# A list schedule that keeps TensorE on products of one kind, whole-array or part-array

## The chip, the cores and the metric

The kernel runs on one core of a Trainium2 chip. The metric is device time in microseconds (us), the median of several executions. The engines of a core work side by side, each through its own instructions in their fixed order: TensorE (PE, matrix products into PSUM), VectorE (DVE), ScalarE (ACT), GpSimd (POOL) and the queue that issues transfers (SP).

## The reference

Two layers over 1,024 tokens of width 1,024, in float32. Each layer modulates and normalizes x, projects it once, runs three mixers side by side on the columns of that projection, projects back and ends with a gated feed-forward part:

```
for l in range(DEPTH):
    mod = jax.nn.silu(c) @ ada_w[l] + ada_b[l]
    ...
    h = rms_norm(x, norm1_g[l]) * (1.0 + sc1) + sh1
    z = h @ w_in[l]
    ...
    o_a = dsa_mixer(...)      # attention to the 256 best keys of an indexer
    o_b = rwkv7_mixer(...)    # a recurrence over the tokens, 8 heads of 64
    o_c = nsa_mixer(...)      # compressed, selected and windowed attention
    mixed = jnp.concatenate([o_a, o_b, o_c], axis=-1) @ w_out[l]
    x = x + g1 * mixed
    h = rms_norm(x, norm2_g[l]) * (1.0 + sc2) + sh2
    gate, up = jnp.split(h @ ffn_wi[l], 2, axis=-1)
    x = x + g2 * ((jax.nn.silu(gate) * up) @ ffn_wo[l])
```

## The kernel before

Tokens are worked in halves of 512, and the work of different halves, mixers and layers is woven together: many generators (streams) yield pieces of work, a planner decides whose piece comes next, and every instruction is recorded with its number in this trace (`r.n`), its engine, its operands and its cost. Buffers in SBUF and PSUM are given out in that step, so what depends on what is fixed by it.

`Program.order()` then makes the final order. It is a list schedule: a model of the chip (`Chip`) says when each engine is free; of the instructions that are ready on an engine, the one with the lowest number in the trace is taken. The engine that can start first goes next, and `Chip.put` moves the model's clock on. The result is one order for each engine; the chip follows it whether or not the model's times were right. An instruction whose operand is late holds up all that stands behind it on its engine.

Products on TensorE come in two kinds for this model. A product has a range of 32-row strips and one of 32-column strips of the 128x128 array (`r.pe`). It is **whole** when it takes four of both, and **part** otherwise. Whole are the projections and the feed-forward (`mm`, three products of float32r halves for each float32 one: `hh`/`hl` by `whi`/`wlo`), the attention scores `at` and the transposes `pt`, `tk`. Part are the products of the recurrence in 64x64 blocks (`X`, `TX`, `WU`, `PT`, `MN`, `S`, `av`, `am`) and in 128x64 (`Y`, the second half of `MN`), attention by values `po` (128x64) and sums over partitions `ssk`, `ss` (128x32). `Chip.start` charges 0.095 us for going from whole to part and 0.045 us for going back, and `Chip.put` another 0.105 us for the first whole one after a part one. So the model knows what a change of kind costs, and the choice among ready products does not look at it.

A part product of the recurrence appears in the profile as two instructions (8 recorded products of `PT` as x16).

Of the kernel before, what the change touches and what calls it, by code (L numbers as in the profile page):

```python
# [88 lines left out]
def consts():  # L89
# [6 lines left out]
    p = np.arange(128)[:, None]  # L96
    f = np.arange(128)[None, :]
    put("ident", p == f)

    put("mask", np.concatenate([np.where(f > p, 0.0, NEG), np.zeros((128, 384)), np.where(f <= p, 0.0, NEG)], 1))  # L100
    put("one", np.ones((128, 1)))
    w = np.arange(32)[None, :]
    put("blkw", p // 64 == w // 16)
# [417 lines left out]
class Program:  # L521
# [83 lines left out]
    def order(self):  # L605


        recs, chip = self.recs, Chip()
        missing = [len(r.deps) for r in recs]
        for r in recs:  # L610
            for d in r.deps:
                recs[d].users.append(r.n)
        ready = {e: [] for e in ENGINES}
        coming = {e: [] for e in ENGINES}
        at = [0.0] * len(recs)
        for r in recs:
            if not missing[r.n]:
                heapq.heappush(coming[r.key], (0.0, r.n))
        out = []
        while len(out) < len(recs):  # L620
            best = None
            for e in ENGINES:
                t = chip.free[e]
                if not ready[e]:
                    if not coming[e]:
                        continue
                    t = max(t, coming[e][0][0])
                while coming[e] and coming[e][0][0] <= t:
                    heapq.heappush(ready[e], heapq.heappop(coming[e])[1])
                n = ready[e][0]  # L630
                s = max(chip.start(recs[n]), at[n])
                if s > t + 0.1 and recs[n].port:

                    for m in heapq.nsmallest(8, ready[e])[1:]:
                        if not recs[m].port and t + recs[m].cost < s + 0.1:
                            n, s = m, max(t, at[m])
                            break
                if best is None or s < best[0]:
                    best = (s, e, n)
            s, e, n = best  # L640
            if ready[e][0] == n:
                heapq.heappop(ready[e])
            else:
                ready[e].remove(n)
                heapq.heapify(ready[e])
            end = chip.put(recs[n], s)
            out.append((s, n))
            for u in recs[n].users:
                v = recs[u]
                at[u] = max(at[u], chip.after(recs[n], v, s, end))  # L650
                missing[u] -= 1
                if not missing[u]:
                    heapq.heappush(coming[v.key], (at[u], u))
        self.span = max(chip.free.values())
        self.starts = {n: s for s, n in out}
        out.sort()
        return [recs[n] for _, n in out]

    def issue(self, tc, order, pools, inputs):
        nc = tc.nc  # L660
        engines = {"PE": nc.tensor, "V": nc.vector, "S": nc.scalar, "G": nc.gpsimd, "D": nc.sync}
        made = {}

        def real(x):
            if not isinstance(x, bass.AP):
                return x
            name = x.tensor.name
            t = made.get(name)
            if t is None:
                b = self.born.get(name)  # L670
                if b is None:
                    t = inputs[name]
                elif b.tag is None:
                    t = pools[b.pool].tile(b.shape, b.dt, name=b.name)
                else:
                    t = pools[b.pool].tile(b.shape, b.dt, name=b.name, tag=b.tag, bufs=1)
                made[name] = t
            h = t.tensor if t.dtype == x.dtype else t.bitcast(x.dtype).tensor
            return bass.AP(tensor=h, offset=x.offset, ap=x.ap)

        with tc.manual_schedule():
            for r in order:
                getattr(engines[r.key], r.name)(*[real(x) for x in r.a], **{n: real(x) for n, x in r.k.items()})  # L683
# [5 lines left out]
class Chip:  # L689
# [5 lines left out]
    def __init__(self):  # L695
# [3 lines left out]
        self.port, self.wire, self.table, self.ring = 0.0, 0.0, None, [0.0] * 8  # L699
        self.stretch, self.work, self.over, self.slow, self.lost = 0, 0.0, 0.0, False, 0.0  # L700

    def start(self, r):

        t = self.free[r.key]
        if r.key == "PE":
            rows, cols, _ = r.pe
            part = rows[1] - rows[0] + cols[1] - cols[0] < 8
            for i in range(*rows):
                t = max(t, max(self.cells[i][cols[0]:cols[1]]))
            return t + (0.0 if part == self.part else 0.095 if part else 0.045)  # L710
        if r.key == "D":
            return max(t, self.ring[0])
        return max(t, self.port - 0.14) if r.port else t

    def put(self, r, s):

        if r.key == "PE":
            rows, cols, c = r.pe
            while s >= (self.stretch + 1) * self.STRETCH:
                share, self.work = (self.work + min(self.over, self.STRETCH)) / self.STRETCH, 0.0  # L720
                self.over = max(0.0, self.over - self.STRETCH)
                self.slow = share < (self.HIGH if self.slow else self.LOW)
                self.stretch += 1
            part = rows[1] - rows[0] + cols[1] - cols[0] < 8
            more = 0.105 if not part and self.first else 0.0

            step = c if not part or r.a[1].dtype != F32 else c / 2 + (0.0 if self.first else 0.05)
            if part and cols[1] - cols[0] == 1:
                step = 0.014
            self.first = part  # L730
            share = 1.0 if not part else (rows[1] - rows[0]) * (cols[1] - cols[0]) / 16.0
            if self.slow:
                self.lost += c * (share if share > 0.3 else 0.3)
                c, step = c * 2, step * 2
            self.work += c if not part else c * max(0.3, share)
            if not part or step < 0.05:
                for i in range(*rows):
                    self.cells[i][cols[0]:cols[1]] = [s + c + more] * (cols[1] - cols[0])
            self.part = part
            self.free["PE"] = s + step + more  # L740
            return s + c
        if r.key == "D":
            self.free["D"] = s + r.cost
            size = r.a[0].free_size() * r.a[0].partition_size() * 4
            self.wire = max(self.wire, s + r.cost) + size / 390e3
            self.ring = self.ring[1:] + [self.wire + 1.5]
            return self.wire + 1.5
        c = r.cost
        if r.func in (AF.Exp, AF.Silu) and r.func != self.table:
            self.table, c = r.func, c + 1.28  # L750
        if r.port:
            self.port = s + c
        self.free[r.key] = s + c - OVER[r.key]
        return s + c
# [17 lines left out]
def trace(ctx: ExitStack, tc: tile.TileContext, A, out, layers=L, plan=None, program=None):  # L772
# [97 lines left out]
    def mm(o, l, r, start=True, stop=True, **kw):  # L870
        o, l, r = flat(o), flat(l), flat(r)
        n = 1
        for x in r.shape[1:]:
            n *= x
        m = l.shape[-1]
        if r.dtype == F32:
            c = 2 * max(2 * n / 2400.0 + (0.0045 if n < 256 else 0.04), m * 0.00083 if m > 32 else 0.05)
        else:
            c = (n if n >= 256 else 4 * n) / 2400.0 + 0.0136
        array(c, (o, l, r), l, l.shape[0], o, m)  # L880
        if program is None:
            PE.matmul(o, l, r, start=start, stop=stop, **kw)
        else:
            program.add("PE", "matmul", (o, l, r), dict(start=start, stop=stop, **kw), (o, l, r), (o,), c, cells)
# [1562 lines left out]
    def mods():  # L2447
        yield from until(("v0",0,0))
        for l in range(layers):
# [7 lines left out]
          [("C", l, b) for b in range(4 * h, 4 * h + 4)] + [("A", l, b) for b in range(4 * h, 4 * h + 4)]]  # L2457
    rq = [(l, p, h) for l in range(layers) for h in range(2) for p in range(4)]
    wv.run((PR["main"], start(0)), (PR["mod"], consts_()), (PR["main"], start(1)), (PR["main"], main()), (PR["mod"], mod_round(0, 0, 16)), *[(PR["att"], att_worker(aq)) for _ in range(NA)],
           (PR["rw"], rw_worker(rq)), (PR["rw2"], rw_worker(rq, lambda t: (t[0], t[2]) in ((0,0),(1,0),(1,1)))),  # L2460
           (PR["mod"], mods()))
# [44 lines left out]
```

## Time and profile before

| what | value |
|---|---|
| median of 3 runs | 3489.34 us (3488.12 to 3493.7) |
| the profiled execution | 3489.09 us |
| its span, first to last instruction | 3487.3 us |
| TensorE busy | 3276.2 us, 94% of the span |
| VectorE busy | 2184.3 us, 63% |
| ScalarE busy | 1781.6 us, 51% |
| GpSimd busy | 1494.4 us, 43% |
| mean granted TensorE clock | 0.97 of full speed |

Busy time of TensorE includes what a product spends in filling and emptying the array. Since products overlap, the time that one costs is read from the start of one to the start of the next.

### The profile page before, as it was taken

How to read it: one execution, taken by the hardware profiler on the slowest of the kernel's cores; microseconds unless marked ns; L12 is line 12 of the kernel's file. 1: busy time of each engine (PE TensorE's matmuls, PEld its weight loads, DVE VectorE, ACT ScalarE, POOL GpSimd, SP SyncE). 2: the span in 40 equal slices, each digit the busy share in tenths (PEclk: the TensorE clock that was granted, in tenths of full speed). 3: DMA queues.
4: the chain of work that ended last, by engine and by line, in shares of the span. 5: the costliest groups of instructions: out<-in, count | busy, mean ns of one | idle time of the engine just before them, and what ended most of it. 6: DMA issues, size and time to landing. Idle time of an engine off the chain costs nothing. (4 is left out here: it accounts for less than half of the span.)

```text
span 3487.3 us, 58649 instructions
## 1 busy us (share of the span) xinstructions
PE 3276.2 (94%) x20564; PEld 2478.0 (71%) x20564; DVE 2184.3 (63%) x5705; ACT 1781.6 (51%) x3708; POOL 1494.4 (43%) x1235
## 2 busy tenths in 40 slices
PE   7889899989999998999899998999899999999999
PEld 3646666766777776677677886667677777778887
DVE  4688878889889624699962114688877843251112
ACT  3445556666674643545563334557777455343232
POOL 3423343433345344453444554443243344445554
PEclk8999999998999998999999999999899999999999
DMA  8674345545623243554223333553222222433333
GB/s 283 196 238 130 90 134 161 156 129 152 200 83 109 66 128 107 151 165 124 75 79 103 97 97 107 152 179 117 63 79 74 75 79 76 134 98 99 97 97 97
DMA packets 354755, 424.99 MB, mean 122 GB/s; under 512 B 129686, under 2 KB 167190, under 8 KB 354460
## 3 DMA queue, kind: packets, MB, share of 16 engines
q1 hardware_dynamic: 354460, 421.25, 39.7%
q8 instruction: 162, 2.65, 0.3%
q14 instruction: 133, 1.09, 0.1%
HBM read 347.06 MB, written 60.44 MB: 117 GB/s over the span
## 5 line engine op out<-in xcount | busy, mean ns | idle before, releaser
L683 POOL TENSOR_TENSOR wlo<-wraw,whi 128x512 fp32r<-128x512 f32 (+1 forms) x808 | 1071.7, 1329 | 1354.7 <-ACT whi L683 1229.3
L683 ACT ACTIVATE whi<-wraw 128x512 fp32r<-128x512 f32 (+1 forms) x808 | 500.7, 621 | 993.9 <-PE mm L683 663.5
L683 PE MATMUL mm<-hh,whi 128*128 128x512 f32 x2144 | 873.7, 409 | 27.6 <-ACT hh L683 10.3
L683 PE MATMUL mm<-hh,wlo 128*128 128x512 f32 x2128 | 845.9, 398 | 7.5 <-POOL wlo L683 7.4
L683 PE MATMUL mm<-hl,whi 128*128 128x512 f32 x2112 | 843.0, 399 | 7.5 <-POOL hl L683 3.8
L683 PEld LDWEIGHTS mm<-hh,whi 128*128 128x128 f32 x2144 | 408.7, 191 | 143.7 <-issue 26.7
L683 PEld LDWEIGHTS mm<-hh,wlo 128*128 128x128 f32 x2128 | 406.3, 191 | 99.9 <-POOL wlo L683 11.7
L683 PEld LDWEIGHTS mm<-hl,whi 128*128 128x128 f32 x2112 | 403.8, 191 | 96.1 <-issue 8.8
L683 DVE TENSOR_TENSOR sg<-sg,mm 128x512 f32<-128x512 f32 x87 | 59.6, 685 | 478.2 <-PE mm L683 478.0
L683 DVE SCALAR_TENSOR_TENSOR x<-mm,mod,x 128x512 f32<-128x512 f32 x232 | 172.9, 747 | 258.6 <-PE mm L683 258.0
L683 PE MATMUL mm<-acthi,whi 128*128 128x512 f32 x704 | 279.4, 402 | 9.3 <-ACT acthi L683 5.0
L683 PE MATMUL mm<-actlo,whi 128*128 128x512 f32 x704 | 277.1, 396 | 2.8 <-POOL actlo L683 2.7
L683 PE MATMUL mm<-acthi,wlo 128*128 128x512 f32 x704 | 275.1, 394 | 0.0
L683 ACT ACTIVATE p<-p,nb,rst 128x512 f32<-128x512 f32 (+3 forms) x256 | 170.7, 668 | 81.7 <-DVE nb L683 80.9
L683 ACT ACTIVATE junka<-score,tk_nt 128x512 int8<-128x512 f32 x240 | 166.4, 693 | 29.0 <-DVE tk_nt L683 22.9
L683 ACT COPY pT<-pt 128x512 f32<-128x512 f32 (+2 forms) x220 | 124.9, 584 | 102.4 <-PE pt L683 96.8
L683 PEld LDWEIGHTS mm<-acthi,whi 128*128 128x128 f32 x704 | 132.6, 189 | 48.7 <-issue 8.0
L683 PEld LDWEIGHTS mm<-actlo,whi 128*128 128x128 f32 x704 | 133.0, 189 | 33.9 <-POOL actlo L683 7.6
L683 DVE TENSOR_SCALAR p<-p,rs 128x512 f32<-128x512 f32 (+3 forms) x288 | 153.7, 586 | 0.7
L683 PEld LDWEIGHTS mm<-acthi,wlo 128*128 128x128 f32 x704 | 133.0, 189 | 27.8 <-issue 0.8
L683 PE MATMUL pt<-c_ident,p 128*128 128x128 f32 x816 | 136.8, 282 | 8.9 <-DVE p L683 7.9
L683 PE MATMUL po<-pT,tm 128*64 128x256 f32 x816 | 132.6, 407 | 6.7 <-ACT pT L683 6.5
(386 smaller groups left out, 5900.8 us busy)
## 6 DMA issues: line engine op xcount, KB each, us to landing
wraw<-in_wi_dram SPq DMA_DIRECT2D x352, 256.0 KB, 2.6
ada<-in_ada_dram SPq DMA_DIRECT2D x192, 256.0 KB, 4.6
wraw<-in_win_dram SPq DMA_DIRECT2D x184, 256.0 KB, 3.1
wraw<-in_wo_dram SPq DMA_DIRECT2D x160, 256.0 KB, 2.6
x<-x SPq DMA_DIRECT2D x64, 256.0 KB, 3.7
w<-in_w_dram SPq DMA_DIRECT2D x64, 256.0 KB, 3.7
wraw<-in_wout_dram SPq DMA_DIRECT2D x64, 256.0 KB, 2.7
o_in<-o SPq DMA_DIRECT2D x32, 256.0 KB, 3.5
```

The costliest lines, as they stand in the source:

```text
L683: getattr(engines[r.key], r.name)(*[real(x) for x in r.a], **{n: real(x) for n, x in r.k.items()})
```

## The change

When the lowest-numbered ready product on TensorE is of the other kind than the last one issued, `order()` now looks for the lowest-numbered ready product of the same kind, and takes it if its number in the trace is at most 100 above. The record of kinds is kept in two heaps, `kinds`; what has been issued is in `begun`. The model's prices, the records, the buffers and what depends on what are as before.

```
-        recs, chip = self.recs, Chip()
+        recs, chip, LATER = self.recs, Chip(), 100
+        kinds, begun = ([], []), set()
...
-                    heapq.heappush(ready[e], heapq.heappop(coming[e])[1])
+                    n = heapq.heappop(coming[e])[1]
+                    heapq.heappush(ready[e], n)
+                    if e == "PE":
+                        heapq.heappush(kinds[Chip.is_part(recs[n])], n)
                 n = ready[e][0]
+                if e == "PE" and Chip.is_part(recs[n]) != chip.part:
+                    same = kinds[chip.part]
+                    while same and same[0] in begun:
+                        heapq.heappop(same)
+                    if same and same[0] - n <= LATER:
+                        n = same[0]
...
+            if e == "PE":
+                begun.add(n)
...
+    @staticmethod
+    def is_part(r):
+        rows, cols, _ = r.pe
+        return rows[1] - rows[0] + cols[1] - cols[0] < 8
```

What this does to the order was counted over all of TensorE's 16,312 recorded products. A return trip is one stretch of part products between whole ones.

| counted in TensorE's order | before | now |
|---|---|---|
| return trips whole, part, whole | 610 | 326 |
| changes from one part shape to another (64x64, 128x64, 128x32, 64x128) | 148 | 266 |

By place in the program, marked by the time at which the same whole products ran before (return trips removed; part-to-part changes added): 0 to 200 us 21; 2. 200 to 1000 us 86; 54. 1000 to 1300 us 44; 20. 1300 to 1500 us 13; 0. 1500 to 1800 us 35; 24. 1800 to 2100 us 4; 0. 2100 to 2550 us 34.5; 7. 2550 to 2900 us 38.5; 11. From 2900 us on 8; 0. A part product stands on average 13 products later in the order than it did, a whole one 5 earlier; nine in ten of the part products are at most 34 places later.

The first place is about 1162 us into the run, on TensorE: `TX` is a part product of the recurrence, `pt` are whole transposes of the attention, and 13 recorded `TX` stand in one row as x13. Before:

```order
4505 L683 MATMUL mm_13433<-hh_9363,whi_13317 128x512
4506 L683 MATMUL TX_13475<-Tt_13297,X_13466 64x64
4507 L683 MATMUL pt_13419<-c_ident,p_13305 128x128
4508 L683 MATMUL TX_13475<-Tt_13297,X_13466 64x64 x2
4509 L683 MATMUL pt_13419<-c_ident,p_13326 128x128
4510 L683 MATMUL TX_13475<-Tt_13297,X_13466 64x64 x13
4511 L683 MATMUL pt_13421<-c_ident,p_13305 128x128
```

The same products of TensorE in the changed kernel:

```order
4515 L697 MATMUL mm_13394<-hh_9360,whi_13424 128x512
4516 L697 MATMUL pt_13472<-c_ident,p_13188 128x128
4517 L697 MATMUL TX_13475<-Tt_13292,X_13461 64x64 x16
4518 L697 MATMUL pt_13455<-c_ident,p_13267 128x128
4519 L697 MATMUL pt_13455<-c_ident,p_13297 128x128
```

Three stretches of `TX` have become one, and two return trips are gone; the transposes that stood between them now follow.

The second place is on TensorE some 20 products on, where attention by values (`po`, 128x64) and the recurrence (`WU` and `PT`, 64x64) are due together. Before, whole transposes stand between them:

```order
4513 L683 MATMUL po_13501<-pT_13484,tm_129 64x256 x2
4514 L683 MATMUL WU_13506<-rhs_12918,Tt_13297 64x128 x8
4515 L683 MATMUL pt_13515<-c_ident,p_13212 128x128
4516 L683 MATMUL pt_13515<-c_ident,p_13274 128x128
4517 L683 MATMUL pt_13515<-c_ident,p_13305 128x128
4518 L683 MATMUL pt_13515<-c_ident,p_13326 128x128
4519 L683 MATMUL po_13501<-pT_13503,tm_129 64x256 x2
4520 L683 MATMUL WU_13526<-rhs_12926,Tt_13297 64x128 x8
```

In the changed kernel:

```order
4536 L697 MATMUL po_13528<-pT_13517,tm_129 64x256 x2
4537 L697 MATMUL WU_13537<-rhs_12876,Tt_13292 64x128 x8
4538 L697 MATMUL po_13528<-pT_13523,tm_129 64x256 x2
4539 L697 MATMUL WU_13554<-rhs_12919,Tt_13292 64x128 x8
4540 L697 MATMUL po_13528<-pT_13530,tm_127 64x256 x2
4541 L697 MATMUL PT_13568<-A_12937,W_13552 64x64
4542 L697 MATMUL po_13528<-pT_13539,tm_127 64x256
```

The part products now follow each other without whole ones between them, in the order of their numbers, so that the two shapes alternate.

The third place is about 1769 us into the run, on TensorE. `PT` and `MN` are part products of the recurrence, `at` are attention scores and `mm` a projection, both whole. Before, `PT` and `MN` stand together:

```order
6949 L683 MATMUL PT_20017<-A_19162,W_19972 64x64
6950 L683 MATMUL PT_20017<-A_19174,W_19972 64x64
6951 L683 MATMUL MN_20029<-bkt_19647,W_19972 64x64 x8
6952 L683 MATMUL MN_20029<-UV_19191,bkt_19647 64x64 x8
6953 L683 MATMUL PT_20051<-A_19177,W_19972 64x64
```

In the changed kernel:

```order
6946 L697 MATMUL WU_20011<-rhs_19153,Tt_19536 64x128 x8
6947 L697 MATMUL PT_20023<-A_19164,W_20005 64x64
6948 L697 MATMUL MN_20025<-bkt_19668,W_20005 64x64
6949 L697 MATMUL at_20027<-K_14176,Qhi_18308 128x512
6950 L697 MATMUL at_20027<-K_14176,Qlo_18327 128x512
6951 L697 MATMUL mm_20030<-hh_19317,whi_19752 128x512
...
6957 L697 MATMUL mm_20030<-hh_19336,whi_19752 128x512
6958 L697 MATMUL PT_20023<-A_19173,W_20005 64x64
```

Here nine whole products have moved in between the first `PT` and the rest of it, and the recurrence's block is finished that much later.

## Rows read from the trace of the kernel before

**Rows 1.** The page's table of busy time, share of the span, instructions.

```profile
span 3487.3 us, 58649 instructions
PE 3276.2 (94%) x20564; PEld 2478.0 (71%) x20564; DVE 2184.3 (63%) x5705; ACT 1781.6 (51%) x3708; POOL 1494.4 (43%) x1235
```

**Rows 2.** Windows by stage: length, busy us of each engine, clock, DMA share, GB/s.

```profile
0.00:200.00 200.00, 161.61 (x789) 103.56 (x789) 120.70 (x301) 84.51 (x162) 79.19 (x79) 0.92 0.76 238
200.00:1000.00 800.00, 738.40 (x5503) 532.99 (x5503) 687.56 (x1922) 483.84 (x1101) 308.44 (x265) 0.96 0.50 150
1000.00:1300.00 300.00, 297.00 (x2052) 224.79 (x2051) 201.33 (x537) 167.59 (x341) 125.49 (x105) 1.00 0.32 95
1300.00:1500.00 200.00, 176.59 (x848) 132.72 (x847) 114.35 (x250) 87.65 (x166) 95.99 (x76) 0.93 0.44 132
1500.00:1800.00 300.00, 284.95 (x2601) 219.61 (x2600) 250.12 (x746) 160.02 (x357) 124.20 (x105) 0.97 0.36 105
1800.00:2100.00 300.00, 300.00 (x1396) 243.63 (x1397) 76.25 (x150) 107.19 (x185) 152.09 (x125) 1.00 0.33 102
2100.00:2550.00 450.00, 406.11 (x2414) 304.46 (x2413) 333.87 (x882) 278.93 (x611) 186.50 (x149) 0.94 0.40 121
2550.00:2900.00 350.00, 342.61 (x2422) 256.34 (x2421) 248.32 (x698) 210.32 (x451) 144.50 (x113) 1.00 0.26 77
2900.00:3488.00 588.00, 568.92 (x2548) 459.88 (x2546) 151.82 (x226) 201.53 (x339) 278.03 (x221) 0.99 0.32 101
```

**Rows 3.** Groups of part products on TensorE: count, busy, mean ns, idle before, releaser.

```profile
L683 PE MATMUL po<-pT,tm 128*64 128x256 f32 x816 | 132.6, 407 | 6.7 <-ACT pT L683 6.5
L683 PE MATMUL X<-Tn,A 64*64 64x64 f32 x1024 | 37.1, 222 | 2.4 <-DVE Tn L683 2.4
```

**Rows 4.** Timeline of TensorE at 1769 us: start us, us until done, instructions.

```profile
1768.39 0.39 PE L683 MATMUL mm<-hl,whi 128*128 128x512 f32 x1
1768.62 0.40 PE L683 MATMUL mm<-hh,wlo 128*128 128x512 f32 x1
1768.95 0.68 PE L683 MATMUL PT<-A,W 64*64 64x64 f32 x16
1769.46 0.63 PE L683 MATMUL MN<-bkt,W 64*64 64x64 f32 x16
1770.03 0.68 PE L683 MATMUL MN<-UV,bkt 128*64 128x64 f32 x16
1770.64 0.68 PE L683 MATMUL PT<-A,W 64*64 64x64 f32 x16
1771.26 0.50 PE L683 MATMUL at<-K,Qhi 128*128 128x512 f32 x1
1771.59 0.40 PE L683 MATMUL at<-K,Qlo 128*128 128x512 f32 x1
1771.92 0.68 PE L683 MATMUL MN<-bkt,W 64*64 64x64 f32 x16
1772.53 0.69 PE L683 MATMUL MN<-UV,bkt 128*64 128x64 f32 x16
```

**Rows 5.** Waits of VectorE from 200 to 1000 us: total us, times, longest.

```profile
DVE p L683 <- PE at L683: 9.4, 12, 2.3
DVE sh L683 <- PE S L683: 6.3, 8, 2.0
```

**Rows 6.** Waits of TensorE, whole run: total us, times, longest.

```profile
PE ss L683 <- DVE nsq L683: 12.6, 5, 5.1
PE mm L683 <- ACT hh L683: 10.3, 7, 3.7
PE mm L683 <- ACT whi L683: 9.1, 4, 4.5
PE rb L683 <- DVE nex L683: 8.5, 3, 4.1
```

More of the change, by code (lines that the diff above doesn't have):

```diff
@@ L706, in start @@
             rows, cols, _ = r.pe
-            part = rows[1] - rows[0] + cols[1] - cols[0] < 8
+            part = self.is_part(r)
             for i in range(*rows):
@@ L723, in put @@
                 self.stretch += 1
-            part = rows[1] - rows[0] + cols[1] - cols[0] < 8
+            part = self.is_part(r)
             more = 0.105 if not part and self.first else 0.0
```

## The prediction

> **What bounds the kernel now.** I read the page's busy times first [rows 1]: TensorE works 3276.2 us of 3487.3, so it stands for 3487.3 - 3276.2 = 211 us, and no other engine reaches two thirds of the span. The reader should take from it that TensorE's order is what matters, and that what is to be gained lies in the way its products follow each other or in those 211 us.
>
> Next come the windows by stage [rows 2], since a share over the whole run hides unlike stretches. In four of them TensorE hardly stands: 3.0 us of 300 from 1000 on, none from 1800, 7.4 of 350 from 2550, 19 of 588 from 2900. These are 1538 us with 29.4 us of standing. In the rest it stands 182 us, and there VectorE is close behind: 687.6 of 800 us (86%) from 200 to 1000, 250 of 300 (83%) from 1500. There the two hold each other up by turns.
>
> Then the waits [rows 6]: they are small and scattered. The largest, of the sums `ss` for the square `nsq`, is 12.6 us in five places, at the norms where a layer begins; nothing stands there that a better order of kinds would shorten. The waits ahead of part products are small too: `po` waits 6.7 us in 816 instructions and `X` 2.4 us in 1,024 [rows 3]. A change of kind is thus mostly paid while TensorE runs without a wait, and is not hidden in one.
>
> What a change of kind costs is not in any busy time; I read it from starts in the timeline [rows 4]. Four prices:
> - A whole product that is followed by a whole one takes 0.23 us to the next start (1768.39 to 1768.62); followed by a part one 0.33 (1768.62 to 1768.95). Leaving whole costs 0.10.
> - `PT` x16 takes 0.51 us when `MN` of the same 64x64 shape follows (1768.95 to 1769.46), and 0.62 when a whole one follows (1770.64 to 1771.26). Leaving a part shape costs 0.11.
> - `MN` x16 takes 0.57 us behind `PT` of its shape (1769.46 to 1770.03), and 0.61 behind a whole one (1771.92 to 1772.53); both leave to another shape. Entering a part shape costs 0.04.
> - The first whole product after part ones takes 0.33 us (1771.26 to 1771.59) in place of 0.23. Entering whole costs 0.10.
>
> A return trip costs 0.10 + 0.04 + 0.11 + 0.10 = 0.35 us. At 1770.03 the shape goes from 64x64 to 128x64 with no whole product between, and `MN` pays for leaving as above; so a change between part shapes costs 0.11 + 0.04 = 0.15 us.
>
> **The change, part by part.** No work is added or taken away; instructions move on every engine, for the schedule of all of them is made anew, but the choice that changed is TensorE's.
>
> Removed: 610 - 326 = 284 return trips, 284 x 0.35 = 99.4 us. The first place in the order shows two of them, `TX` split by single transposes.
>
> Added: 266 - 148 = 118 changes between part shapes, 118 x 0.15 = 17.7 us. The second place in the order shows how they arise: with the transposes gone from between them, `po` and `WU` alternate. The model knows only whole and part, so it sees no price there; by its own view the gain would be 99.4 us.
>
> The Trainium skill (TensorEngine Tiling (Array Packing), section Key Properties) says that changing the tiling mode drains TensorE, while changing only the tile does not; by that rule the model's free changes among part shapes are not free. The trace agrees: `PT` to `MN` in one shape 0.51 us, from one part shape to another as dear as to a whole one.
>
> Saved on TensorE: 99.4 - 17.7 = 81.7 us. It is the most that the step can bring, if every removed change ends work sooner.
>
> Where does it land? In the four stretches where TensorE hardly stands, the counts are 44 + 4 + 38.5 + 8 = 94.5 return trips and 20 + 0 + 11 + 0 = 31 part-to-part changes: 94.5 x 0.35 - 31 x 0.15 = 28.4 us. I take all of it, since there is always a next product ready. The remaining 81.7 - 28.4 = 53.3 us lie in stretches where TensorE stands for 182 us and VectorE is busy up to 86%. If VectorE and its chains alone set the pace there, nothing is gained; if TensorE alone, everything. The trace of before can't show how the schedule will share it; as TensorE is still the busier of the two (738 against 688 us from 200 to 1000), and VectorE waits for it only in small pieces, 9.4 us for scores and 6.3 us for `S` [rows 5], I take half, 26.6 us, and keep both ends for the range.
>
> Moved: a part product stands 13 places later on average, and 13 x 0.23 = 3.0 us is my estimate of its delay, from the step of a whole product [rows 4]. Behind it wait the copies out of PSUM on ScalarE and VectorE and then the next product of the same chain; the third place in the order shows such a case, where nine whole products (about 2 us) stand inside `PT`. Ahead of the part products come whole ones that have to be done anyway, so this delay takes no time while TensorE has other work. The cover is that stock of whole products; where it runs out, at the norms and in the recurrence from 200 to 1000, a delay of 3 us is a wait of up to 3 us. The limit of 100 numbers holds it down: a product can't fall behind further and further, so the delay does not grow along a chain as long as the trace itself leaves room. I put it at nothing in the sum beyond the half already taken off. The transfers and weight splits move with the whole products, which come 5 places, about 1 us, earlier; a wait for `whi` costs 9.1 us in all now [rows 6], and I see no reason for it to double.
>
> The clock I leave at 0.97. It was full in the stretches without standing and 0.92 to 0.94 where TensorE stood most [rows 2]; the products are the same, so it should move only with the standing.
>
> Sum: 28.4 + 26.6 = 55.0 us. Against the profiled execution's 3489.1 us (1.8 us outside its span) that is 3434 us. The median of the runs, 3489.34, differs from it by 0.3 us.
>
> **The rivals.**
> - All of it lands: the mixed stretches give their whole 53.3 us too. For it speaks that TensorE is the busiest engine in every stretch; against it, 86% of VectorE. 3489 - 82 = 3407 us.
> - The gain is swallowed: in the mixed stretches chains through VectorE and ScalarE set the pace, TensorE merely stands longer, and part of the saving in the full stretches comes back as standing at the next norm. Half of 28.4 remains: 3475 us. For it speak the 182 us of standing that are there now.
> - It doesn't do what it says: the drains removed reappear as waits of other kinds one for one, or the new orders of VectorE and ScalarE cost what TensorE saves. Within 0.2% of 3489, which is 7 us and about what a measurement of this kernel tells from no change.
> - Slower: delayed part products of the recurrence stand on the chain from 200 to 1000, where VectorE has 112 us to spare and TensorE 62. With 3.0 us for each delayed product on which the chain waits, 82 / 3.0 = 27 such places eat the whole gain, and with 40 of them it is 120 - 82 = 38 us slower: 3527 us. Against it speaks the limit of 100, and that only 8 waits of VectorE for `S` are in that stretch now.
>
> **How the numbers follow.** Forecast, 3415 to 3460: 0.50. All of it, below 3415: 0.13. Swallowed, 3460 to 3482: 0.18. Within 0.2%, 3482 to 3496: 0.08. Slower: 0.11. So faster by over 0.2% has 0.50 + 0.13 + 0.18 = 0.81. The likeliest is 3434 us. The range for 8 in 10 goes from 3403 (all of it, with the prices 5% higher, as they are read to 0.01 us) to 3476 (swallowed), which leaves out the no-change and slower cases, 0.19, and a little of the others.
>
> **What would show it.** In the profile of the changed kernel: starts in the timeline at the same prices (0.33 for a whole product next to part ones); from 1000 to 1300 the same products done some 12 us sooner; TensorE's standing near 211 us plus the half not gained, some 238 us; the mean clock between 0.96 and 0.98. Wrong would be: standing of TensorE above 290 us, with waits for VectorE or ScalarE ahead of `am`, `X`, `S` or `po` of 30 us and more; or a step between products of one kind that differs from 0.23.

## The result, and the profile after

The changed kernel takes 3441.42 us (median of 4 runs, 3437.63 to 3443.23) against 3488.73 of before: a ratio of 0.9861, 95% interval 0.9844 to 0.9879. That is 47 us less; 3434 was forecast, with a range from 3403 to 3476.

The page's table of busy time of the changed kernel, which answers to [rows 1]:

```profile
span 3441.0 us, 58566 instructions
PE 3215.3 (93%) x20564; PEld 2496.7 (73%) x20564; DVE 2176.2 (63%) x5705; ACT 1775.1 (52%) x3706; POOL 1488.3 (43%) x1235
```

The same products take 60.9 us less of TensorE's busy time, and TensorE stands for 3441.0 - 3215.3 = 225.7 us, 14.6 more than before: 60.9 - 14.6 = 46.3 us, the difference of the two spans.

The windows by stage of the changed kernel, as [rows 2] (length, busy us of PE, PEld, DVE, ACT and POOL, clock, DMA share, GB/s):

```profile
0.00:200.00 200.00, 159.46 (x793) 107.51 (x793) 112.75 (x289) 84.42 (x161) 79.56 (x79) 0.90 0.77 244
200.00:1000.00 800.00, 740.61 (x5583) 550.34 (x5584) 703.25 (x1983) 488.26 (x1121) 318.98 (x268) 0.96 0.49 150
1000.00:1300.00 300.00, 295.93 (x2077) 234.58 (x2076) 192.35 (x495) 163.42 (x329) 135.31 (x111) 1.00 0.32 99
1300.00:1500.00 200.00, 171.57 (x852) 133.71 (x851) 124.16 (x296) 93.46 (x183) 94.38 (x78) 0.91 0.47 144
1500.00:1800.00 300.00, 278.87 (x2615) 217.77 (x2614) 245.16 (x728) 160.43 (x353) 118.50 (x102) 0.95 0.33 95
2550.00:2900.00 350.00, 346.11 (x2366) 271.86 (x2366) 247.48 (x660) 211.87 (x440) 139.36 (x112) 1.00 0.27 81
```

The stages have moved forward a little, so these are not quite the same products; the reader should look at standing and clock. From 1500 to 1800, where the recurrence is densest, TensorE now stands for 21.1 us in place of 15.1, and the clock is 0.95 in place of 0.97; at 0 to 200 and 1300 to 1500 the clock is 0.02 lower as well. The view of the cores gives the mean:

```profile
core 0: 3441.0 us, clock 0.965
```

It was 0.970. As the clock has two levels, full and half, the span less its mean share is what half the clock can have cost at most: 0.035 x 3441 = 120 us now, 0.030 x 3487 = 105 before, 16 us more (an upper bound, since part of that time TensorE stood anyway). One execution is thin ground for this: the other three of the changed kernel have 0.967 to 0.970.

The timeline of TensorE of the changed kernel shows the prices of [rows 4] again, to within 0.02 us, and a wait (start us, us until done, instructions, and in brackets the idle time before):

```profile
1135.13 0.39 PE L697 MATMUL mm<-hl,whi 128*128 128x512 f32 x1
1135.36 0.39 PE L697 MATMUL mm<-hh,wlo 128*128 128x512 f32 x1
1135.67 1.15 PE L697 MATMUL X<-Tn,A 64*64 64x64 f32 x32
1136.75 0.50 PE L697 MATMUL mm<-hh,whi 128*128 128x512 f32 x1
1137.09 0.39 PE L697 MATMUL mm<-hl,whi 128*128 128x512 f32 x1
...
1139.38 0.39 PE L697 MATMUL mm<-hh,wlo 128*128 128x512 f32 x1
1141.04 1.15 PE L697 MATMUL TX<-X,Tt 64*64 64x64 f32 x32 [1.27 <-ACT X L697]
```

0.23 between whole products, 0.31 to leave whole, 0.34 for the first whole one after `X`: the steps forecast. Then `TX`, the next product of the same chain, stands 1.27 us for ScalarE's copy of `X`. The same view of ScalarE shows why that copy is late:

```profile
1137.87 0.80 ACT L697 ACTIVATE p<-p,nb,rst 128x512 f32<-128x512 f32 x1
...
1140.42 0.56 ACT L697 COPY X<-X 128x512 f32<-128x512 f32 x1
```

`X` was done at 1136.82, and ScalarE, which has the attention's `p` ahead of the copy in its order, worked on that until 1140.4. So this wait comes from ScalarE's order, and not from a delay of `X` on TensorE. The groups of part products in the recurrence show what waits there are ahead of them (busy us, mean ns, idle before, releaser):

```profile
L697 PE MATMUL po<-pT,tm 128*64 128x256 f32 x816 | 114.0, 392 | 5.6 <-ACT pT L697 5.5
L697 PE MATMUL X<-Tn,A 64*64 64x64 f32 x1024 | 37.5, 223 | 5.2 <-DVE ex L697 4.6 <-DVE Tn L697 0.6
L697 PE MATMUL S<-sh,MT 64*64 64x64 f32 x416 | 34.8, 243 | 5.4 <-DVE sh L697 5.4
```

`po` is busy for 114.0 us where it was 132.6 [rows 3], since its stretches are longer (188 stretches of 128x64 products in the order, 264 before); `X` waits 5.2 us where it waited 2.4. The wait of TensorE that grew most stands ahead of whole products, `mm` for VectorE's `z` (total us, times, longest); in order, before, the changed kernel, and the tenth experiment below:

```profile
PE mm L683 <- DVE z L683: 1.5, 2, 1.2
PE mm L697 <- DVE z L697: 10.5, 6, 6.4
PE mm L700 <- DVE z L700: 10.0, 4, 7.1
```

The tenth experiment has it too and loses almost nothing, so this wait alone is not what the changed kernel loses.

### The profile page after: what moved, and what is told of

Same layout as the page of the kernel before. It is cut to its first block, busy times and chain, and to the rows that moved or that the text cites. A ratio compares the mean times of both kernels' runs of the same rounds, so it can differ in the third digit from the quotient of the medians.

```text
span 3441.0 us, 58566 instructions
## 1 busy us (share of the span) xinstructions
PE 3215.3 (93%) x20564; PEld 2496.7 (73%) x20564; DVE 2176.2 (63%) x5705; ACT 1775.1 (52%) x3706; POOL 1488.3 (43%) x1235
## 5 line engine op out<-in xcount | busy, mean ns | idle before, releaser
L697 PE MATMUL mm<-hh,whi 128*128 128x512 f32 x2144 | 865.9, 405 | 38.5 <-ACT hh L697 10.4
L697 PEld LDWEIGHTS mm<-hl,whi 128*128 128x128 f32 x2112 | 404.3, 191 | 94.6 <-issue 8.2
L697 PEld LDWEIGHTS pt<-c_ident,p 128*128 128x128 f32 x816 | 100.9, 143 | 48.8 <-issue 11.8
```

## The experiments

The theory after the result: the drains are worth what was counted, 82 us, and some 35 us of it are eaten by something. Two candidates: VectorE and its chains set the pace in the mixed stretches, as the prediction's half had it; or the delay of the part products, which the prediction had put at nothing. Rivals to both: the gain is a chance of the new order; and a change between part shapes is free. "Drains" below means return trips at 0.35 us and part-to-part changes at 0.15 us, counted in TensorE's order. The gains are (1 - ratio) x 3489 us; an interval of a ratio is about 7 us to each side.

**Only where TensorE hardly stood.**

```
+        FULL = ((8714, 11209), (15583, 17464), (21063, 30000))
-                if e == "PE" and Chip.is_part(recs[n]) != chip.part:
+                if e == "PE" and Chip.is_part(recs[n]) != chip.part and any(a <= n < b for a, b in FULL):
```

> The rule is in force only for records of the stretches in which TensorE hardly stood (numbers 8714 to 11209, 15583 to 17464 and from 21063 on). The order then has 513 return trips and 179 part-to-part changes (before: 610 and 148), which at 0.35 and 0.15 us is 97 x 0.35 - 31 x 0.15 = 29.3 us. Theory A (the drains, taken whole where TensorE is saturated): 3489 - 29 = 3460 us. Rival B (swallowed: the time comes back as standing at the next norm, half is lost): 3474 us. Rival C (the gain of the changed kernel is a lucky new order, not the drains): no tie to the count, about 3489 us give or take 15.

3459.78 us, ratio 0.9905 (0.9887 to 0.9924): 33 us gained of 29 counted. All of it lands, and nothing is swallowed at the next norm.

**Only in the other stretches** (`and not any(...)`).

> The complement: the rule is in force only for records of the other stretches. 418 return trips and 232 part-to-part changes: 192 x 0.35 - 84 x 0.15 = 54.6 us of drains. Theory A (half of it lands): 3489 - 27 = 3462 us. All lands: 3434 us. Rival (delay of the part products hurts where VectorE is close behind): nothing gained or slower, 3485 to 3500 us.

3473.44 us, ratio 0.9949 (0.9930 to 0.9967): 18 us of 55, a third. The two parts together give 51 us, the whole rule 48; what is lost is lost here.

**A shorter reach.**

```
-        recs, chip, LATER = self.recs, Chip(), 100
+        recs, chip, LATER = self.recs, Chip(), 30
```

> LATER 30 in place of 100. 408 return trips and 246 part-to-part changes: 202 x 0.35 - 98 x 0.15 = 56.0 us of drains, and part products stand 4 places later on average in place of 13. If drains alone decide and the same share of them lands as in the changed kernel (47 of 82): 3489 - 32 = 3457 us. If the share that did not land was eaten by the delay of part products, less delay leaves more: 3489 - 48 = 3441 us, level with the changed kernel.

3448.72 us, ratio 0.9873 (0.9854 to 0.9892): 44 us of 56. With fewer drains saved it is level with the changed kernel, as the delay has it; drains with a fixed share would have been 12 us off.

**By shape.** The heap is kept for each shape of the array as well, and the choice looks there first.

```
+                    for same in (shapes.get(chip.shape, []), kinds[chip.part]):
...
+                        if same and same[0] - n <= LATER:
+                            n = same[0]
+                            break
```

> The rule looks first for a ready product of the same array shape within 100, then for one of the same kind. 329 return trips and 200 part-to-part changes against 326 and 266 of the changed kernel: 66 x 0.15 - 3 x 0.35 = 8.9 us fewer drains. If a change between part shapes costs 0.15 us and the same share lands (47 of 82): 3441 - 5 = 3436 us; if all lands: 3432 us. If such changes are free, as the schedule's model has it: 3441 us or 1 us more.

3431.17 us, ratio 0.9824 (0.9805 to 0.9843): 61 us of 91, 13 us better than the changed kernel. The interval of that difference is some 9 us to each side; it speaks against a free change between part shapes, and can't tell 0.15 us from somewhat more. Grouping by shape also puts more products side by side that use different parts of the array (see the reverse below); the run does not tell the two apart.

**A long reach** (`LATER` 400).

> LATER 400 in place of 100. 269 return trips and 313 part-to-part changes: 341 x 0.35 - 165 x 0.15 = 94.6 us of drains, 13 us more than the changed kernel; but part products stand 73 places later on average in place of 13. Drains alone, 47 of 82 landing: 3489 - 54 = 3435 us. If delay is what eats the rest, and grows with the places (13 places cost 82 - 47 = 35 us), it is slower than the changed kernel and could lose everything: 3489 - 95 + 35 x 73 / 13 = 3590 us; the limit would then be what keeps the change faster.

3504.92 us, ratio 1.0030 (1.0014 to 1.0046): with the most drains saved of all, 95 us, it is slower than before. 105 us are lost. The line through zero that I drew from 13 places was too steep at 73, but the sign and the order of size are those of the delay. The page and the clock of this kernel:

```profile
span 3508.5 us, 58565 instructions
PE 3242.8 (92%) x20564; PEld 2526.2 (72%) x20564; DVE 2152.0 (61%) x5705; ACT 1788.8 (51%) x3716; POOL 1482.0 (42%) x1235
...
core 0: 3508.5 us, clock 0.954
```

Standing is 265.7 us, 55 more than before, and 0.046 x 3508.5 = 161 us is the bound for the clock, 57 more. VectorE is less busy than it was (61%), so its load does not set the pace.

**A blind mark as a control.** The kind is `n // 16 % 2` in place of whole and part.

> Control: the same rule with the same reach of 100, but the kind is a mark that has nothing to do with the array (whether the record's number divided by 16 is even or odd). The order is stirred about as much (part products 13 places away from before on average, 18 in the changed kernel), and the count is 704 return trips and 191 part-to-part changes: 94 x 0.35 + 43 x 0.15 = 39.4 us more drains than before. Theory A: slower, between 3489 + 23 = 3512 us (the share that landed) and 3528 us (all). Rival C (any new order with a reach of 100 does it): 3441 us or near.

3611.05 us, ratio 1.0339 (1.0320 to 1.0358): 118 us slower. So stirring the order gained nothing by itself here; with the first experiment, whose gain follows the count, this speaks against the chance of a new order as the cause. But it loses far more than 39 us of drains; standing is 3604.0 - 3356.4 = 247.6 us, 36 more. TensorE is busy 3356.4 - 3276.2 = 80.2 us longer, of which the count leaves 41 us unexplained, with a clock that is not lower (0.973); this is left open.

**The reverse.** The rule takes the other kind, with a reach of 4.

```
-                if e == "PE" and Chip.is_part(recs[n]) != chip.part:
-                    same = kinds[chip.part]
+                if e == "PE" and Chip.is_part(recs[n]) == chip.part:
+                    same = kinds[not chip.part]
```

> The reverse: the rule takes a ready product of the other kind if its number is at most 4 above. 1322 return trips and 103 part-to-part changes: 712 x 0.35 - 45 x 0.15 = 242 us more drains than before, with almost no delay of part products (4 places away on average). Theory A: 3489 + 242 = 3731 us if each trip costs 0.35 us; standing that is there already can take up some of it, so 3650 to 3731 us. If drains hide behind other engines: within 50 us of 3489.

3880.62 us in one run, 391 us slower than the profiled execution of before: more than 242. Standing is 27 us longer, the clock's bound 47. The timeline of this kernel shows what else:

```profile
1251.60 0.65 PE L697 MATMUL po<-pT,tm 128*64 128x256 f32 x2
1252.17 0.33 PE L697 MATMUL pt<-c_ident,p 128*128 128x128 f32 x1
1252.43 0.65 PE L697 MATMUL po<-pT,tm 128*64 128x256 f32 x2
1253.01 0.44 PE L697 MATMUL pt<-c_ident,p 128*128 128x128 f32 x2
```

Two `po` instructions, which are one recorded product, take 0.57 us to the next start. In the changed kernel four take 0.58:

```profile
1150.05 0.65 PE L697 MATMUL po<-pT,tm 128*64 128x256 f32 x4
1150.63 1.09 PE L697 MATMUL WU<-rhs,Tt 64*64 64x128 f32 x16
```

Recorded `po` products take one half of the array's columns or the other (`r.pe`), and two of different halves that stand together run side by side; where the reverse rule parts them, it pays for both in turn, on top of the trip. The group of all `po` shows it:

```profile
L697 PE MATMUL po<-pT,tm 128*64 128x256 f32 x816 | 217.4, 409 | 16.0 <-ACT pT L697 16.0
```

It is busy for 217.4 us, where it was 132.6 before [rows 3].

**Holding on to part products only.**

```
-                if e == "PE" and Chip.is_part(recs[n]) != chip.part:
+                if e == "PE" and chip.part and not Chip.is_part(recs[n]):
```

> Half of the rule: it holds on to part products only, never to whole ones. 460 return trips and 254 part-to-part changes: 150 x 0.35 - 106 x 0.15 = 36.6 us of drains, and part products stand 3 places earlier than before, not 13 later. If drains alone decide with 47 of 82 landing: 3489 - 21 = 3468 us. If the delay of part products took the rest, it is not there now: 3489 - 37 = 3452 us or less.

3449.2 us, ratio 0.9883 (0.9864 to 0.9902): 41 us of 37. All of it lands, in the mixed stretches too (25 of the 37 are counted there), with less than half of the changed kernel's drains saved.

**Holding on to whole products only** (`not chip.part and Chip.is_part(recs[n])`).

> The other half of the rule: it holds on to whole products only (reach 100), never to part ones. 326 return trips and 286 part-to-part changes: 284 x 0.35 - 138 x 0.15 = 78.7 us of drains; part products stand 14 places later, as in the changed kernel. If that delay is what ate the rest there (82 - 47 = 35 us), this one loses as much: 3490 - 79 + 35 = 3446 us. If delay costs nothing: 3411 us. If holding on to whole is what loses everything: 3490 us.

3446.89 us, ratio 0.9859 (0.9840 to 0.9879): 49 us of 79. As far as the intervals tell, the loss of the changed kernel is all in this half.

**Long behind part, short behind whole.** By shape, with

```
-        recs, chip, LATER = self.recs, Chip(), 100
+        recs, chip, LATER, WHOLE = self.recs, Chip(), 100, 30
...
-                        if same and same[0] - n <= LATER:
+                        if same and same[0] - n <= (LATER if chip.part else WHOLE):
```

> By shape as in the fourth experiment, but the reach is 100 when the last product was a part one and 30 when it was whole. 376 return trips and 177 part-to-part changes: 234 x 0.35 - 29 x 0.15 = 77.6 us of drains, 13 us fewer saved than by shape with reach 100 both ways; part products stand where they did (0.6 places earlier on average, in place of 13 later). If the delay ate the rest, nearly all lands: 3490 - 78 = 3412 us, faster than the changed kernel and than the one by shape. If drains alone decide, with the share of the changed kernel (47 of 82): 3490 - 45 = 3445 us.

3417.43 us, ratio 0.9781 (0.9764 to 0.9798): 76 us of 78. Against by shape only the reach behind whole products differs: 13 us fewer are counted and 15 us more gained. The page and the clock:

```profile
span 3414.1 us, 58611 instructions
PE 3192.3 (94%) x20564; PEld 2473.9 (72%) x20564; DVE 2181.7 (64%) x5705; ACT 1780.6 (52%) x3712; POOL 1488.3 (44%) x1235
...
core 0: 3414.1 us, clock 0.973
```

83.9 us less busy time than before, standing 221.8 us (11 more), and the clock is not lower.

**A reach of 15 behind whole.**

> The same with a reach of 15 behind a whole product. 395 return trips and 182 part-to-part changes: 215 x 0.35 - 34 x 0.15 = 70.2 us of drains; part products stand 2 places earlier than before. By the drains with nothing lost: 3420 us, 7 us slower than with 30; if the reach of 30 still costs delay, this one is level with it or faster.

3433.27 us, ratio 0.9823 (0.9804 to 0.9842): 62 us of 70, slower than with 30. What a reach of 30 delays costs less than what it saves.

**A reach of 100 behind whole only where TensorE hardly stood.**

> As the tenth experiment (by shape, reach 100 behind part and 30 behind whole), but behind whole the reach is 100 for records of the stretches in which TensorE hardly stood. 358 return trips and 181 part-to-part changes: 252 x 0.35 - 33 x 0.15 = 83.2 us of drains, 5.7 us more than there. If the delay of part products is free where TensorE never waits: 5 to 6 us faster than the tenth, a ratio of 0.976. If delay costs there too: level with it or slower, 0.978 to 0.982.

3408.36 us, ratio 0.9769 (0.9748 to 0.9789): 81 us of 83, the fastest of all kernels here. It is 4 us better than the tenth, which the intervals do not tell from level; that delay is free where TensorE is saturated rests on the first experiment.

Put together, in us; "standing" and "clock" (the bound) are changes against before in the profiled execution, "places" is how much later part products stand in the order on average:

| kernel | drains | gain | not landed | standing | clock | places |
|---|---|---|---|---|---|---|
| the change | 82 | 48 | 33 | +15 | +16 | 13 |
| only where saturated | 29 | 33 | -4 | -5 | +6 | 4 |
| only elsewhere | 55 | 18 | 37 | +19 | +24 | 9 |
| reach 30 | 56 | 44 | 12 | +4 | +2 | 4 |
| by shape | 91 | 61 | 29 | +18 | +15 | 13 |
| reach 400 | 95 | -10 | 105 | +55 | +57 | 73 |
| part only | 37 | 41 | -4 | -5 | -12 | -3 |
| whole only | 79 | 49 | 30 | +27 | +13 | 14 |
| part 100, whole 30 | 78 | 76 | 1 | +11 | -12 | -1 |
| part 100, whole 15 | 70 | 62 | 8 | +5 | -2 | -2 |
| part 100, whole 30 or 100 | 83 | 81 | 3 | -1 | +1 | 3 |

What did not land is the sum of the two columns beside it, to within some 13 us in every row. Standing is in that sum by arithmetic, since a span is busy time and standing. What tests the count is the busy time: it fell by the drains less the clock's column, to within 11 us in every row (the change: 60.9 us, against 81.7 - 15.8 = 65.9; reach 400: 33.4, against 94.6 - 56.8 = 37.8). So the drains were saved in all these kernels, and what is lost comes back as standing and as work at half the clock. The blind mark and the reverse are not in the table; there the count leaves 41 us and some 75 us unexplained, the latter at least in part by groups cut in two.

The clock's column is of one execution each, and executions of one kernel differ: before has 0.965 to 0.973 in the 42 that were timed beside the experiments. An entry of some 10 us says little by itself; reach 400 (0.954 to 0.958 in ten executions) lies clear of it.

What did not land goes roughly with the places: it is largest by far at 73, and small from -3 to 4; between them it is not in order (37 at 9, 33 at 13). That the cost comes from holding on to whole products for long is shown by the two halves of the rule and by the reaches. The path, from a late part product through the copies and VectorE back to TensorE, is argued: no one wait in the traces carries the loss.

## Why the prediction was right, and where it was not

**The prices and the count held.** In five kernels nearly everything that was counted was gained (33 of 29, 41 of 37, 76 of 78, 62 of 70, 81 of 83), with the prices read from one stretch of 4 us of the timeline.

**All of it lands where TensorE is saturated.** With the rule in force only there, so it was: 33 us measured alone, 28.4 in the sum. Within the changed kernel it is less clear. Matched product by product between the two traces, and averaged over the products within 25 us of each mark, TensorE's products come 19 us sooner at 1000 us of before, 25 at 1300, 27 at 1500, 17 at 1800, 20 at 2100, 32 at 2550, 47 at 2900 and 47 at the end. That is an estimate, good to some 3 us, as products have changed places. It gives 23 us in the four saturated stretches and 24 in the others, where 28.4 and 26.6 were forecast. The sign named for 1000 to 1300, the same products some 12 us sooner, came out at 6 us, and from 1500 to 1800 the kernel gives some of its lead back.

**Half of it lands elsewhere.** The term was 26.6 us; measured alone it is 18, with an interval of 7 to each side, so it was somewhat too large. Its reason was wrong. I took half because VectorE is nearly as busy there and would share the pace. If that were the limit, no order of TensorE could gain more there; yet the tenth kernel gains 76 us over the whole run, of 78 counted, 52 of them in the mixed stretches, with VectorE's work unchanged (2181.7 us, before 2184.3).

**The delay put at nothing is the step that failed.** The sum has no term for it beyond the half already taken off for VectorE. The prediction held that whole products that come ahead "have to be done anyway" and that the limit of 100 numbers holds the delay down. The second half of the sentence is right in kind, and 100 is too much in size: the loss is all in holding on to whole products, shrinks with a reach of 30 and grows past the whole gain with 400. What the slower rival of the prediction named, a price for delayed part products, is thus real; in the changed kernel some 33 us are lost, and with a reach of 400 more than the whole gain. That they stand on the chain from 200 to 1000, as that rival has it, is not shown; by the estimate above, that stretch kept most of its gain.

**The clock left at 0.97** was close: 0.965 in the profiled execution, 0.965 to 0.970 in all four, inside the band from 0.96 to 0.98 that was named. In the profiled execution it costs up to 16 us, and standing is 226 us, not the 238 forecast: part of what was lost there went into half the clock. The prediction said that the clock should move only with the standing. In most rows of the table they move together, and the consequence, that standing can bring about as much again, was not drawn.

**A price between part shapes** was right to be counted as far as the runs tell: by shape is 13 us better than the change, of which 9 were counted, and more products side by side may have a share in it. What the prediction says beside it, that by the model's own view the gain would be 99.4 us, is wrong: by the charges of `Chip`, 0.095 + 0.045 + 0.105 = 0.245 us for a trip, 284 trips are some 70 us. Nothing in the sum rests on it.

That the result fell 7 us from the forecast is in part luck: the 26.6 us taken off for VectorE, for a reason that did not hold, were nearly as large as the 33 us of loss that were left out.

## What to carry to other kernels

Where an engine pays for a change of mode, count the changes in its order and read the price from starts in the timeline, at four points: leaving and entering, on both sides. Grouping is worth nearly the whole count as long as it does not hold back the work that others wait for: hold on to the chain's short products for long, and to the bulk that fills the gaps only briefly. One number for both directions gave 48 us here, 61 when grouped by shape; two numbers, by shape, gave 76.

## What the runs showed of the hardware that was not expected

**Standing can be paid twice.** Here the clock fell after TensorE had stood, and stayed at half through the work that came then. The windows of the changed kernel around the longest such stretch (length, busy us of PE, PEld, DVE, ACT and POOL, clock, DMA share, GB/s):

```profile
733.90:740.70 6.80, 6.60 (x43) 4.76 (x38) 6.46 (x20) 5.88 (x14) 2.55 (x3) 1.00 0.83 262
740.80:747.60 6.80, 3.33 (x20) 2.01 (x19) 6.80 (x21) 1.26 (x2) 3.80 (x4) 1.00 0.74 232
747.70:781.60 33.90, 21.74 (x82) 15.79 (x82) 32.44 (x73) 12.59 (x26) 11.55 (x10) 0.50 0.33 101
```

TensorE stands for 3.5 of 6.8 us at full clock; then it has half the clock, 1.2 GHz in place of 2.4, for 33.9 us, of which it works 21.74, so about 10.9 us of work at full speed took twice as long. In most rows of the table the two columns move together, most clearly with a reach of 400 (+55 and +57); part 100, whole 30 is an exception, with 11 us more standing and a clock that is not lower.

**Grouped part products share the array.** Two `po` instructions cost 0.57 us and four 0.58; a group of four that is cut in two costs twice, beside the trip. A price of a trip measured on whole groups is too low for an order that cuts them.

The Trainium skill (TensorEngine Tiling (Array Packing), section Key Properties) says that tiles operate independently and that a change of mode drains TensorE. The trace agrees with both (four `po` in the time of two, and 0.35 us for a return trip [rows 4]).
